# Six adaLN pieces of the second block: from TensorE chunks in the first half's up-projection to row products on GpSimd and ScalarE

## The chip, the cores and the metric

The kernel runs on one core of a Trainium2 chip. The metric is device time of one execution in microseconds (us), as the median of several runs. Besides, one execution was taken by the hardware profiler; all durations below come from it. Its engines are named PE (TensorE), PEld (PE's weight loads), DVE (VectorE), ACT (ScalarE), POOL (GpSimd) and SP (the sync engine, which here only issues DMAs). Each engine works through its own list of instructions in order.

## The reference, cut to what matters

Two layers on 256 context and 256 latent tokens of width 1024. Each layer computes six adaLN vectors per conditioning vector, and they scale and shift every norm and gate every residual:

```
mod_l = (silu(c) @ mod_w[layer] + mod_b[layer])       # 6 x 1024 values for the latent tokens
mod_c = (silu(c_ctx) @ mod_w[layer] + mod_b[layer])   # the same for the context tokens
sh1, sc1, g1, sh2, sc2, g2 = split(mod, 6)
h = rmsnorm(x, norm_mix_g) * (1 + sc1) + sh1 ;  x = x + g1 * mixer(h)
h = rmsnorm(x, norm_ffn_g) * (1 + sc2) + sh2 ;  x = x + g2 * conv_ffn(h)
```

The second layer is the last one, so from `g1` on it needs the latent vector alone. `conv_ffn` is an up-projection to 2 x 2816 channels, a depthwise convolution, SiLU gating and a down-projection.

## The kernel before, in words

Activations lie transposed: 128 channels on the partitions, 512 tokens along a row (`xT`, eight tiles). Every large product is made of three matmuls on split operands: a weight unit of eight 128x128 blocks is loaded by SP into `raw`, rounded by ACT into `wh` (L173), and the rest is formed into `wl` by DVE or POOL (L174). `Stream` does this one unit ahead; `wp` keeps four units. A unit of eight blocks serves 24 matmuls of 512 columns (L185 to L187).

A chunk (`mod_chunk(l, j)`) makes 512 columns of the adaLN product: two loads of 1 MB, eight matmuls with a 32-column operand (L244), a copy by ACT (L261), four transposes (L264), and two or three small DVE operations. Twelve chunks make a layer; chunks 4 and 5 of layer 1 are `g1`, 6 and 7 are `sh2`, 8 and 9 are `sc2`. In the kernel before, nine chunks of layer 1 are taken from the list `fill1` by the first feed-forward's up-projection, one for each 16 blocks from the third load on.

The first feed-forward has two halves. In each, eleven steps `project(jj)` make a gate tile and a value tile (two units of weights, 48 matmuls), `centre` copies each off the accumulators (ACT, L792), DVE adds the other taps (L798), ACT and POOL finish the gating (L816, L819, L822, L823); then comes that half's down-projection.

Ahead of it stands the first out-projection (`WO`, eight units): four row tiles together, then four one by one. After each, DVE adds the residual (L334), ACT squares it (L286) and DVE adds up the squares (L288); after the eighth square follow a column sum on PE, a chain of small DVE operations, the transposes of L140 and the copy of the result on ACT (`rstd`, L141). Only then can the norm (L315, L321, L323) feed the up-projection.

What order the instructions take on each engine is decided by a scheduler when the program is built: it goes by dependencies and by its own durations, not by the source's order alone. It is fixed in the built program.

Of the kernel before, what the change touches and what calls it, by code (L numbers as in the profile page):

```python
# [51 lines left out]
def block_kernel(ctx: ExitStack, tc: tile.TileContext, A: dict, out: bass.AP):  # L52
# [91 lines left out]
    class Stream:  # L144
        def __init__(self, src, nblocks, fill=None, every=1, skip=0, ahead=1, pool=rawp, eng=lambda u: v, parts=wp):


            self.src, self.n, self.ahead, self.parts = src, nblocks, ahead, parts
            self.fill, self.every, self.skip, self.pool, self.eng = fill, every, skip, pool, eng
            self.raw = self.rawi = None  # L150
            self.units = {}

        def load(self, d):
# [10 lines left out]
        def split(self, u):  # L164
            self.load(u // 2)
            if u == 1:
                nc.sync.dma_start(out=self.raw[:, 1024:], in_=self.src[0, :, 1024:])
            n = min(8, self.n - u * 8) * P
            o = (u % 2) * 1024
            hi = self.parts.tile([P, 1024], F32R, tag="wh", name=nm("wh"))  # L170
            lo = self.parts.tile([P, 1024], F32R, tag="wl", name=nm("wl"))
            rw = self.raw[:, o:o + n]
            s.activation(out=hi[:, :n], in_=rw, func=AF.Copy)  # L173
            self.eng(u).tensor_tensor(out=lo[:, :n], in0=rw, in1=hi[:, :n].bitcast(F32), op=ALU.subtract)  # L174
            self.units[u] = (hi, lo)

        def get(self, b):
            u = b // 8
# [79 lines left out]
    def mod_out(l, c, n, ps, psa):  # L258

        ev = t2((P, n * P))  # L260
        s.copy(out=ev, in_=ps)  # L261
        pt = psa()[:, :n * P].rearrange("p (a b) -> p a b", b=P)
        for a in range(n):
            te.transpose(pt[:, a, :], ev[:, a * P:(a + 1) * P], ident)  # L264
        col = lambda name, o: pc(name, o, n).unsqueeze(2).to_broadcast([P, n, 2])
        i, k = c // KD, c % KD
        dst = comps[l][i][:, k:k + n, :]
        v.tensor_reduce(out=dst, in_=pt.rearrange("p a (q c) -> p a c q", q=4)[:, :, 0:2, :], axis=AX.X, op=ALU.add)
        v.tensor_tensor(out=dst, in0=dst, in1=col("modb", l * 48 + c), op=ALU.add)
        if i in (1, 4):  # L270

            v.scalar_tensor_tensor(out=dst, in0=dst, scalar=1.0, in1=col("nmg" if i == 1 else "nfg", l * 8 + k), op0=ALU.add, op1=ALU.mult)

    accs = np_.tile([P, T], F32, tag="acc", name="acc", bufs=1)

# [100 lines left out]

        acts = norm_mod(0, 0, 1, SEGS, r, start)
    fill0 = [lambda j=j: mod_chunk(0, j) for j in (4, 5, 8, 9, 6, 7)]
    fill1 = [lambda j=j: mod_chunk(1, j) for j in (3, 0, 1, 4, 5, 8, 9, 6, 7, 11)]
    E.fill0, E.W0 = fill0, W0  # L380
    nrm = Norm(0, T)
    with ExitStack() as st:
        even_mixer(E, st, acts, pss0, nrm.add)
    for k in range(KD):
        dump(f"x1_{k}", xT[k])
    r = nrm.row()
    mod_chunk(1, 2, rawp, mps)
    acts = norm_mod(0, 3, 4, SEGS, r)
    with ExitStack() as st:
        hs, nrms = [], [Norm(a, b) for _, a, b in SEGS]  # L390

        def then(m, sgs):
            for sg in sgs:
                nrms[sg[0]].add(m)
                if m == KD - 1:
                    hs[:] = hs or [htiles(k) for k in range(KD)]
                    norm_mod(1, 0, 1, (sg,), nrms[sg[0]].row(), tiles=hs)

        conv_ffn(E, st, acts, fill1[:-1], then)
    for k in range(KD):  # L400
        dump(f"x2_{k}", xT[k])
    with ExitStack() as st:
# [8 lines left out]
        last_ffn(E, st, acts, fill1[-1:], out)  # L411


def even_mixer(E, st, acts, pss0, then):
    nc, tc, A = E.nc, E.tc, E.A
    v, s, g, te = E.v, E.s, E.g, E.te
    pc, nm, mps, dump, ident, ones = E.pc, E.nm, E.mps, E.dump, E.ident, E.ones
# [348 lines left out]
    finish(3)  # L766
    for k in range(8):
        dump(f"m{k}", hh[k].bitcast(F32))
    WO = E.Stream(A["wout0"], 64)
# [56 lines left out]
def conv_ffn(E, st, acts, fill, then):  # L826

    v, g = E.v, E.g
    cv = Conv(E, st, 0, T)
# [1 line left out]
    up = E.Stream(E.A["up0"], 44 * KD, fill, 1, 2, pool=ur, eng=lambda u: g)  # L831
    first = []
    per = FF // 2
    dn = E.Stream(E.A["dn0"], FF * KD, eng=lambda u: g if u * 8 % (per * KD) < per * 4 else v)

    def project(j):
        if j == 0:
# [10 lines left out]
    for hf in range(2):  # L848
# [6 lines left out]
        for jj in range(per):  # L855
            cg, ca = nxt
            if jj < per - 1:
                nxt = project(hf * per + jj + 1)

            if jj == per - 2:  # L860
                done = jj - 1
                pss = E.gemm_k(dn, b0, per, oa, [(0, T)] * 4, pss, range(done))
            h, part = cv.tile(cg, ca, g, part, jj)
            hm.append(h)
        part()
        last = hf == 1
# [4 lines left out]
        for m in range(4, KD - 2 if last else KD):  # L871
            E.residual(0, 5, m, E.gemm_f(dn, b0 + m * per, per, oa), SEGS)
            if last:
                then(m, SEGS)

    for sg in SEGS:
        for m in (KD - 2, KD - 1):
# [373 lines left out]
def layout(inp):  # L1251
# [2 lines left out]
    xx = np.concatenate([f["ctx"][0], f["x"][0]], 0)  # L1254
    A["x"] = xx.T.reshape(KD, P, T).transpose(1, 0, 2).reshape(P, KD * T)
    A["cv"] = np.stack([f["c_ctx"], f["c"][0]], -1).reshape(KD, P, 2).transpose(1, 0, 2).reshape(P, 16)
    A["mods"] = f["mod_w"][0][:, :2048].reshape(KD, P, 8, 256).transpose(2, 1, 0, 3).reshape(8, P, 2048)
    A["modw"] = f["mod_w"].reshape(2, KD, P, 12, 512).transpose(0, 3, 2, 1, 4).reshape(2, 12, P, 4096)
    prm = np.zeros((P, NPRM), np.float32)
# [106 lines left out]
```

## Time before, and its profile

| | us |
|---|---|
| median of three runs (1280.5 to 1283.16) | 1280.86 |
| the profiled execution | 1282.09 |
| its span, first to last instruction | 1280.3 |
| PE busy | 1227.8 (96%) |
| DVE, ACT, POOL busy | 926.0, 594.4, 428.8 |

The profiled execution is 1.23 us above the median; 1.8 us of it lie outside the span.

### The profile page before, as it was taken

How to read it: one execution, taken by the hardware profiler on the slowest of the kernel's cores; microseconds unless marked ns; L12 is line 12 of the kernel's file. 1: busy time of each engine (PE TensorE's matmuls, PEld its weight loads, DVE VectorE, ACT ScalarE, POOL GpSimd, SP SyncE). 2: the span in 40 equal slices, each digit the busy share in tenths (PEclk: the TensorE clock that was granted, in tenths of full speed). 3: DMA queues.
4: the chain of work that ended last, by engine and by line, in shares of the span. 5: the costliest groups of instructions: out<-in, count | busy, mean ns of one | idle time of the engine just before them, and what ended most of it. 6: DMA issues, size and time to landing. Idle time of an engine off the chain costs nothing.

```text
span 1280.3 us, 18746 instructions
## 1 busy us (share of the span) xinstructions
PE 1227.8 (96%) x7094; PEld 1003.9 (78%) x7094; DVE 926.0 (72%) x2061; ACT 594.4 (46%) x937; POOL 428.8 (33%) x249
## 2 busy tenths in 40 slices
PE   7989999999999999999999999999999998999995
PEld 5657787876867777888888897888888897899994
DVE  4483889487658776227785478888888956989995
ACT  4463345344344333223443346666666645555543
POOL 0100000000225565326666000032222224999974
PEclk8999999999999999999999999999999998999998
DMA  9557202334536564222211225453544376555521
GB/s 372 200 187 234 107 22 78 129 107 165 172 130 263 202 259 166 99 99 99 99 66 66 99 75 147 142 168 124 165 131 125 108 270 218 193 172 191 178 91 61
DMA packets 40106, 191.45 MB, mean 150 GB/s; under 512 B 4608, under 2 KB 10568, under 8 KB 21072
## 3 DMA queue, kind: packets, MB, share of 16 engines
q1 hardware_dynamic: 36512, 185.48, 41.6%
q10 hardware_dynamic: 3504, 4.77, 1.2%
q8 instruction: 56, 0.92, 0.3%
q14 instruction: 34, 0.28, 0.1%
HBM read 189.03 MB, written 1.20 MB: 149 GB/s over the span
## 4 chain that ended last, share of the span: by engine, by line
PE 75%; DVE 10%; issue 4%; DMA 4%; ACT 4%; POOL 2%; SPq 0%; DVEq 0%; ACTq 0%; POOLq 0%
PE gps L185 12%; PE gps L186 12%; PE gps L187 12%; PE mps L185 6%; PE mps L187 6%; PE mps L186 6%; PE vps L244 3%; PE gps L932 1%; PE vps L1174 1%; PE gps L933 1%; PE gps L931 1%; POOL wl L174 1%; PE gps L220 1%; PE gps L222 1%; PE gps L221 1%
## 5 line engine op out<-in xcount | busy, mean ns | idle before, releaser
L174 POOL TENSOR_TENSOR wl<-raw,wh 128x1024 fp32r<-128x1024 f32 x122 | 293.6, 2415 | 495.7 <-ACT wh L173 459.4
L173 ACT ACTIVATE wh<-raw 128x1024 fp32r<-128x1024 f32 x226 | 237.4, 1054 | 170.8 <-PE gps L187 99.6
L185 PE MATMUL gps<-hh,wh 128*128 128x512 f32 (+1 forms) x824 | 290.8, 354 | 6.7 <-ACT hh L321 4.9
L186 PE MATMUL gps<-hh,wl 128*128 128x512 f32 (+1 forms) x824 | 289.6, 352 | 1.1 <-DVE wl L174 1.1
L187 PE MATMUL gps<-hl,wh 128*128 128x512 f32 (+1 forms) x824 | 290.2, 353 | 0.0
L798 DVE SCALAR_TENSOR_TENSOR y<-mps,fcw,y 128x255 f32<-128x255 f32 (+3 forms) x592 | 247.5, 433 | 51.7 <-ACT y L792 37.5
L185 PEld LDWEIGHTS gps<-hh,wh 128*128 128x128 f32 x824 | 155.6, 189 | 41.7 <-issue 12.5
L174 DVE TENSOR_TENSOR wl<-raw,wh 128x1024 fp32r<-128x1024 f32 x104 | 127.6, 1234 | 79.6 <-ACT wh L173 79.4
L185 PE MATMUL mps<-hh,wh 128*128 128x256 f32 (+1 forms) x544 | 178.2, 328 | 0.0
L187 PE MATMUL mps<-hl,wh 128*128 128x256 f32 (+1 forms) x544 | 176.5, 325 | 1.6 <-DVE hl L323 1.6
L186 PE MATMUL mps<-hh,wl 128*128 128x256 f32 (+1 forms) x544 | 177.0, 325 | 0.0
L186 PEld LDWEIGHTS gps<-hh,wl 128*128 128x128 f32 x824 | 156.1, 189 | 23.2 <-issue 3.2
L187 PEld LDWEIGHTS gps<-hl,wh 128*128 128x128 f32 x824 | 156.0, 190 | 20.8 <-issue 1.7
L185 PEld LDWEIGHTS mps<-hh,wh 128*128 128x128 f32 x544 | 105.4, 194 | 16.9 <-issue 6.7
L187 PEld LDWEIGHTS mps<-hl,wh 128*128 128x128 f32 x544 | 105.2, 194 | 9.2 <-DVE hl L323 1.8
L186 PEld LDWEIGHTS mps<-hh,wl 128*128 128x128 f32 x544 | 105.6, 194 | 7.8
L798 DVE SCALAR_TENSOR_TENSOR y<-gps,fcw,y 128x189 f32<-128x189 f32 (+3 forms) x180 | 77.7, 438 | 22.0 <-ACT y L792 18.2
L792 ACT ACTIVATE y<-mps,fcw 128x256 f32<-128x256 f32 (+1 forms) x68 | 41.2, 637 | 91.5 <-PE mps L187 91.5
L185 PE MATMUL gps<-mh,wh 128*128 128x512 f32 (+1 forms) x198 | 73.5, 371 | 0.0
L187 PE MATMUL gps<-ml,wh 128*128 128x512 f32 (+1 forms) x198 | 73.4, 371 | 0.0
L186 PE MATMUL gps<-mh,wl 128*128 128x512 f32 (+1 forms) x198 | 73.4, 370 | 0.0
L334 DVE SCALAR_TENSOR_TENSOR x<-gps,mod,x 128x256 f32<-128x256 f32 x56 | 24.2, 478 | 42.0 <-PE gps L187 42.0
(292 smaller groups left out, 1894.0 us busy)
## 6 DMA issues: line engine op xcount, KB each, us to landing
raw<-in_up SPq DMA_DIRECT2D x42, 1024.0 KB, 4.9
rawm<-in_modw SPq DMA_DIRECT2D x36, 1024.0 KB, 6.6
raw<-in_win SPq DMA_DIRECT2D x32, 1024.0 KB, 5.4
raw<-in_dn SPq DMA_DIRECT2D x20, 1024.0 KB, 5.1
raw<-in_wout SPq DMA_DIRECT2D x10, 1024.0 KB, 5.6
rawm<-in_mods SPq DMA_DIRECT2D x8, 1024.0 KB, 14.5
R<-crd SPq DMA_DIRECT2D x32, 256.0 KB, 4.2
rawm<-in_modw SPq DMA_DIRECT2D x8, 512.0 KB, 5.0
```

What stands on the lines that cost most here:

```text
L173: s.activation(out=hi[:, :n], in_=rw, func=AF.Copy)
L174: self.eng(u).tensor_tensor(out=lo[:, :n], in0=rw, in1=hi[:, :n].bitcast(F32), op=ALU.subtract)
L185: te.matmul(out=ps, lhsT=lhi, rhs=rhi, start=first, stop=False)
L186: te.matmul(out=ps, lhsT=llo, rhs=rhi, start=False, stop=False)
L187: te.matmul(out=ps, lhsT=lhi, rhs=rlo, start=False, stop=last)
L220: te.matmul(out=ps, lhsT=ah[:, sl], rhs=hi[:, c:c + 512], start=k == 0, stop=False)
L221: te.matmul(out=ps, lhsT=ah[:, sl], rhs=lo[:, c:c + 512], start=False, stop=False)
L222: te.matmul(out=ps, lhsT=al[:, sl], rhs=hi[:, c:c + 512], start=False, stop=k == nk - 1)
L244: te.matmul(out=ps[32 * (k % 4):32 * (k % 4) + 32, :], lhsT=spad[:, k, :], rhs=raw[:, kk * 512:(kk + 1) * 512], start=k < 4, stop=k >= 4)
L334: v.scalar_tensor_tensor(out=xT[m][:, a:b], in0=ps[:, a - base:b - base], scalar=gt[:, m, ci:ci + 1], in1=xT[m][:, a:b], op0=ALU.mult, op1 ...
L792: self.E.s.activation(out=y, in_=ps, func=AF.Identity, scale=self.fcw[:, c + 4:c + 5], bias=self.fcw[:, c + 9:c + 10])
L798: self.E.v.scalar_tensor_tensor(out=o, in0=i, scalar=self.fcw[:, ti * 10 + wi:ti * 10 + wi + 1], in1=o, op0=ALU.mult, op1=ALU.add)
```

## The change

Chunks 4 to 9 of layer 1 leave `fill1`. In their place the class `Rows` makes these 3072 values for the latent vector in 24 pieces of 128: `start()` loads `c` to all partitions (`row`), forms silu(c) there with ACT and POOL, and each `step()` does three things for three pieces: ACT sums the products of one piece along its row (an activation copy with a summing output, L299), SP loads 512 KB of transposed weights for a new piece (`wt`, two buffers, L308), and POOL multiplies the loaded piece by `row` (L313). `start` and the steps hang on units of the first out-projection (6 steps), on units of both halves' down-projection and on odd steps of the second half's up-projection; what is left is made at the end. The out-projection moves out of the mixer's scope, so that the new pool takes over memory of the mixer. In each half two more units of the down-projection are split by DVE in place of POOL.

```diff
+            if self.aside:
+                self.aside(u)
...
+        def start(self):
+            pool = self.pool
+            self.row = pool.tile([P, D], F32, tag="row", name="row")
+            nc.sync.dma_start(out=self.row, in_=A["crow"].to_broadcast([P, D]))
+            th = pool.tile([P, D], F32, tag="wt", name=nm("wt"), bufs=2)
+            s.activation(out=th, in_=self.row, func=AF.Tanh, scale=0.5)
+            g.tensor_scalar(out=th, in0=th, scalar1=0.5, scalar2=0.5, op0=ALU.mult, op1=ALU.add)
+            g.tensor_tensor(out=self.row, in0=self.row, in1=th, op=ALU.mult)
...
+                s.activation(out=w, in_=w, func=AF.Copy, accum_out=dst[:, k, 1:2])
...
+                w = self.pool.tile([P, D], F32, tag="wt", name=nm("wt"), bufs=2)
+                nc.sync.dma_start(out=w, in_=A["modt"][self.c])
...
+                g.tensor_tensor(out=self.made[1], in0=self.made[1], in1=self.row, op=ALU.mult)
...
-    fill1 = [lambda j=j: mod_chunk(1, j) for j in (3, 0, 1, 4, 5, 8, 9, 6, 7, 11)]
+    fill1 = [lambda j=j: mod_chunk(1, j) for j in (3, 0, 1, 11)]
...
+    WO.aside = lambda u: rows.start() if u == 1 else rows.step() if u > 1 else None
...
-    dn = E.Stream(E.A["dn0"], FF * KD, eng=lambda u: g if u * 8 % (per * KD) < per * 4 else v)
+    dn = E.Stream(E.A["dn0"], FF * KD, eng=lambda u: g if u % per < 4 else v)
+    dn.aside = lambda u: rows.step() if u % per >= 4 else None
...
+            if jj % 2 and hf:
+                rows.step()
...
+    rows.finish()
```

ACT at the end of the out-projection, before: `wh` are rounded weight units of the up-projection (`raw_3152` its first load), `t<-x` the squares of residual tiles 4 to 7 (x_95 the last), then a chunk's copy and `rstd`.

```order
L286 ACTIVATE t_547_2906<-x_92 128x512
L173 ACTIVATE wh_3159<-raw_3152 128x1024
L286 ACTIVATE t_552_2942<-x_93 128x512
L173 ACTIVATE wh_3189<-raw_3187 128x1024
L286 ACTIVATE t_556_2976<-x_94 128x512
L173 ACTIVATE wh_3217<-raw_3187 128x1024
L286 ACTIVATE t_558_3006<-x_95 128x512
L261 COPY t_569_3055<-mps_3042 128x512
L141 COPY rstd_3022<-vps_3036 128x512
```

The same place now, from the square of tile 5; L299 sums a piece, and the squares' line is L332.

```order
L332 ACTIVATE t_558_2970<-x_93 128x512
L299 ACTIVATE wt_2941,mod_2_114<-wt_2941 128x1024
L299 ACTIVATE wt_2979,mod_2_114<-wt_2979 128x1024
L173 ACTIVATE wh_3219<-raw_3217 128x1024
L332 ACTIVATE t_563_3008<-x_94 128x512
L299 ACTIVATE wt_4293,mod_2_114<-wt_4293 128x1024
L173 ACTIVATE wh_3247<-raw_3217 128x1024
L299 ACTIVATE wt_4378,mod_2_114<-wt_4378 128x1024
L332 ACTIVATE t_565_3038<-x_95 128x512
L263 COPY t_576_3085<-mps_3072 128x512
L299 ACTIVATE wt_4412,mod_3_115<-wt_4412 128x1024
L141 COPY rstd_3052<-vps_3066 128x512
```

Eight sums stand ahead of the last square and a ninth ahead of `rstd`; `wt_4293`, `wt_4378` and `wt_4412` hang on the first half's down-projection in the source.

POOL from its first work of this stretch, before: the rests of the up-projection's first units.

```order
L174 TENSOR_TENSOR wl_3155<-raw_3152,wh_3154 128x1024
L174 TENSOR_TENSOR wl_3160<-raw_3152,wh_3159 128x1024
L174 TENSOR_TENSOR wl_3190<-raw_3187,wh_3189 128x1024
L174 TENSOR_TENSOR wl_3218<-raw_3187,wh_3217 128x1024
L174 TENSOR_TENSOR wl_3271<-raw_3245,wh_3270 128x1024
```

POOL at the same place now: the row of silu(c) (L290, L291), then products of pieces (L313) between those rests.

```order
L290 TENSOR_SCALAR wt_2752<-wt_2752 128x1024
L291 TENSOR_TENSOR row<-row,wt_2752 128x1024
L313 TENSOR_TENSOR wt_2786<-wt_2786,row 128x1024
L313 TENSOR_TENSOR wt_2816<-wt_2816,row 128x1024
L174 TENSOR_TENSOR wl_3185<-raw_3182,wh_3184 128x1024
L313 TENSOR_TENSOR wt_2850<-wt_2850,row 128x1024
L313 TENSOR_TENSOR wt_2901<-wt_2901,row 128x1024
L174 TENSOR_TENSOR wl_3190<-raw_3182,wh_3189 128x1024
L313 TENSOR_TENSOR wt_2941<-wt_2941,row 128x1024
L313 TENSOR_TENSOR wt_2979<-wt_2979,row 128x1024
L174 TENSOR_TENSOR wl_3220<-raw_3217,wh_3219 128x1024
L313 TENSOR_TENSOR wt_4293<-wt_4293,row 128x1024
```

Two products stand before each rest of a unit; further down the list the 24th and last product stands ahead of the rest of the up-projection's sixteenth unit, in the first half.

ACT between the norm and the first `centre` copies of the up-projection, before: two roundings, a chunk's copy, then the copies.

```order
L173 ACTIVATE wh_3332<-raw_3245 128x1024
L173 ACTIVATE wh_3385<-raw_3361 128x1024
L261 COPY t_614_3260<-vps_3247 128x512
L792 ACTIVATE y_3298<-gps_3148,fcw_3143 128x512
L792 ACTIVATE y_3300<-mps_3149,fcw_3143 128x512
```

The same place now, where the copies' line is L847 and the chunk's copy L263.

```order
L299 ACTIVATE wt_4454,mod_3_115<-wt_4454 128x1024
L173 ACTIVATE wh_3362<-raw_3275 128x1024
L299 ACTIVATE wt_4491,mod_3_115<-wt_4491 128x1024
L299 ACTIVATE wt_4523,mod_3_115<-wt_4523 128x1024
L173 ACTIVATE wh_3415<-raw_3391 128x1024
L263 COPY t_621_3290<-vps_3277 128x512
L847 ACTIVATE y_3328<-gps_3178,fcw_3173 128x512
L299 ACTIVATE wt_4560,mod_3_115<-wt_4560 128x1024
L847 ACTIVATE y_3330<-mps_3179,fcw_3173 128x512
```

Three sums now stand ahead of the chunk's copy, and a fourth between the first two `centre` copies.

## Rows read from the trace of the kernel before

**Rows 1.** The page: the span, busy time of each engine.

```profile
span 1280.3 us, 18746 instructions
PE 1227.8 (96%) x7094; PEld 1003.9 (78%) x7094; DVE 926.0 (72%) x2061; ACT 594.4 (46%) x937; POOL 428.8 (33%) x249
```

**Rows 2.** Windows: start:end, length, busy of PE, PEld, DVE, ACT, POOL; clock, DMA.

```profile
440.00:460.00 20.00, 20.00 (x99) 15.15 (x98) 12.80 (x31) 7.25 (x10) 9.79 (x5) 1.00 0.52 203
...
540.00:560.00 20.00, 20.00 (x87) 16.10 (x86) 5.37 (x8) 4.25 (x4) 1.39 (x1) 1.00 0.31 105
...
600.00:620.00 20.00, 20.00 (x90) 16.53 (x89) 15.58 (x37) 8.99 (x12) 12.99 (x9) 1.00 0.30 105
```

**Rows 3.** Timeline, ACT: start, duration; `centre` copies in the first and second half.

```profile
455.61 0.78 ACT L792 ACTIVATE y<-mps,fcw 128x512 f32<-128x512 f32 x1 [1.02 <-PE mps L187]
...
469.07 0.78 ACT L792 ACTIVATE y<-mps,fcw 128x512 f32<-128x512 f32 x1 [1.02 <-PE mps L187]
...
590.49 0.78 ACT L792 ACTIVATE y<-mps,fcw 128x512 f32<-128x512 f32 x1 [3.19 <-PE mps L187]
...
601.37 0.78 ACT L792 ACTIVATE y<-mps,fcw 128x512 f32<-128x512 f32 x1 [3.19 <-PE mps L187]
```

**Rows 4.** Timeline, PE: a chunk inside the up-projection.

```profile
447.48 1.92 PE L244 MATMUL vps<-rawm,spad 128*32 128x512 f32 x16
449.33 0.50 PE L185 MATMUL mps<-hh,wh 128*128 128x512 f32 x1
```

**Rows 5.** Timeline, SP: the up-projection's first load.

```profile
320.51 0.33 SPq L159 DMA_DIRECT2D raw<-in_up  x1
```

**Rows 6.** DMA issues: KB each, median us from issue to landing.

```profile
raw<-in_win SPq DMA_DIRECT2D x6, 512.0 KB, 3.5
...
raw<-in_wout SPq DMA_DIRECT2D x4, 512.0 KB, 4.4
...
raw<-in_dn SPq DMA_DIRECT2D x4, 512.0 KB, 5.8
```

**Rows 7.** Lines by form, POOL and ACT: count, busy, mean ns, idle before.

```profile
L174 POOL TENSOR_TENSOR wl<-raw,wh 128x1024 fp32r<-128x1024 f32 x122 | 293.6, 2415 | 495.7 <-ACT wh L173 459.4 <-DVE acc L288 33.1 <-issue 2.1
L823 POOL TENSOR_TENSOR ml<-y,mh 128x512 fp32r<-128x512 f32 x22 | 28.6, 1301 | 2.2 <-ACT mh L822 2.2
...
L1163 POOL TENSOR_TENSOR CE<-CE 128x256 f32<-128x256 f32 x16 | 24.1, 1508 | 63.2 <-DVE CE L1162 63.2
L823 POOL TENSOR_TENSOR ml<-y,mh 128x256 fp32r<-128x256 f32 x22 | 16.3, 741 | 7.6 <-ACT mh L822 7.6
...
L1038 POOL TENSOR_SCALAR cl<-cl 128x256 f32<-128x256 f32 x4 | 3.5, 880 | 111.2 <-DVE cum L1063 82.1 <-PE mps L1032 29.1
```

**Rows 8.** Timeline, ACT: from the out-projection's last squares to the first chunk's copy.

```profile
337.04 1.06 ACT L173 ACTIVATE wh<-raw 128x1024 fp32r<-128x1024 f32 x1 [3.02 <-PE gps L187]
...
353.37 1.06 ACT L173 ACTIVATE wh<-raw 128x1024 fp32r<-128x1024 f32 x1 [3.87 <-PE gps L187]
354.34 0.61 ACT L286 ACTIVATE t<-x 128x512 f32<-128x512 f32 x1
...
359.85 0.59 ACT L141 COPY rstd<-vps 128x512 f32<-128x512 f32 x1 [1.07 <-PE vps L140]
...
376.02 0.51 ACT L321 ACTIVATE hh<-t,mod 128x256 fp32r<-128x256 f32 x1 [0.28 <-DVE t L315]
...
382.15 0.59 ACT L261 COPY t<-vps 128x512 f32<-128x512 f32 x1 [0.83 <-PE vps L244]
```

**Rows 9.** Timelines, DVE and POOL: an addition of squares without and beside POOL's work.

```profile
335.09 0.69 DVE L288 TENSOR_TENSOR acc<-acc,t 128x512 f32<-128x512 f32 x1
...
338.65 2.54 DVE L288 TENSOR_TENSOR acc<-acc,t 128x512 f32<-128x512 f32 x1 [0.79 <-ACT t L286]
...
338.24 2.40 POOL L174 TENSOR_TENSOR wl<-raw,wh 128x1024 fp32r<-128x1024 f32 x1 [286.77 <-ACT wh L173]
```

**Rows 10.** Timeline, PE: the first chunk's transposes in the up-projection.

```profile
383.01 0.60 PE L264 MATMUL vps<-c,t 128*128 128x128 f32 x4
```

More of the change, by code (lines that the diff above doesn't have):

```diff
@@ L149, in __init__ @@
             self.fill, self.every, self.skip, self.pool, self.eng = fill, every, skip, pool, eng
-            self.raw = self.rawi = None
+            self.raw = self.rawi = self.aside = None
             self.units = {}
@@ L272, in mod_out, with __init__, step, finish @@
             v.scalar_tensor_tensor(out=dst, in0=dst, scalar=1.0, in1=col("nmg" if i == 1 else "nfg", l * 8 + k), op0=ALU.add, op1=ALU.mult)
+    class Rows:
+        N = 3 * KD
+        def __init__(self, pool):
+            self.pool, self.c, self.loaded, self.made = pool, 0, None, None
+        def start(self):
[6 more added lines that the diff above has]
+            g.tensor_tensor(out=self.row, in0=self.row, in1=th, op=ALU.mult)
+        def step(self):
+            if self.made is not None:
+                c, w = self.made
+                i, k = 2 + c // KD, c % KD
+                dst = comps[1][i]
+                s.activation(out=w, in_=w, func=AF.Copy, accum_out=dst[:, k, 1:2])
+                if k == KD - 1:
+                    d = dst[:, :, 1]
+                    v.tensor_tensor(out=d, in0=d, in1=pc("modb", 48 + 8 * i, 8), op=ALU.add)
+                    if i == 4:
+                        v.scalar_tensor_tensor(out=d, in0=d, scalar=1.0, in1=pc("nfg", 8, 8), op0=ALU.add, op1=ALU.mult)
+            new = None
+            if self.c < self.N:
+                w = self.pool.tile([P, D], F32, tag="wt", name=nm("wt"), bufs=2)
+                nc.sync.dma_start(out=w, in_=A["modt"][self.c])
+                new = (self.c, w)
+                self.c += 1
+            self.made = self.loaded
+            if self.made is not None:
+                g.tensor_tensor(out=self.made[1], in0=self.made[1], in1=self.row, op=ALU.mult)
+            self.loaded = new
+        def finish(self):
+            while self.loaded or self.made:
+                self.step()
     accs = np_.tile([P, T], F32, tag="acc", name="acc", bufs=1)
@@ L382, in block_kernel @@
     with ExitStack() as st:
-        even_mixer(E, st, acts, pss0, nrm.add)
+        hh, hl = even_mixer(E, st, acts, pss0)
+    mst = ExitStack()
+    rows = Rows(mst.enter_context(tc.tile_pool(name="mw", bufs=1)))
+    even_out(E, hh, hl, nrm.add, rows)
     for k in range(KD):
@@ L388, in block_kernel @@
     acts = norm_mod(0, 3, 4, SEGS, r)
-    with ExitStack() as st:
+    with mst, ExitStack() as st:
         hs, nrms = [], [Norm(a, b) for _, a, b in SEGS]
@@ L397, in then @@
                     norm_mod(1, 0, 1, (sg,), nrms[sg[0]].row(), tiles=hs)
-        conv_ffn(E, st, acts, fill1[:-1], then)
+        conv_ffn(E, st, acts, fill1[:-1], then, rows)
     for k in range(KD):
@@ L411, in block_kernel, with even_mixer @@
         last_ffn(E, st, acts, fill1[-1:], out)
-def even_mixer(E, st, acts, pss0, then):
+def even_mixer(E, st, acts, pss0):
     nc, tc, A = E.nc, E.tc, E.A
@@ L768, in even_mixer, with even_out @@
         dump(f"m{k}", hh[k].bitcast(F32))
-    WO = E.Stream(A["wout0"], 64)
+    return hh, hl
+def even_out(E, hh, hl, then, rows):
+    WO = E.Stream(E.A["wout0"], 64)
+    WO.aside = lambda u: rows.start() if u == 1 else rows.step() if u > 1 else None
     oa = lambda k: (hh[k], hl[k])
@@ L823, in tile, with conv_ffn @@
         return (h_, l_), lambda: self.E.g.tensor_tensor(out=l_, in0=ya, in1=h_.bitcast(F32), op=ALU.subtract)
-def conv_ffn(E, st, acts, fill, then):
+def conv_ffn(E, st, acts, fill, then, rows):
     v, g = E.v, E.g
@@ L1256, in layout @@
     A["cv"] = np.stack([f["c_ctx"], f["c"][0]], -1).reshape(KD, P, 2).transpose(1, 0, 2).reshape(P, 16)
+    A["crow"] = f["c"].reshape(1, D)
+    A["modt"] = f["mod_w"][1][:, 2048:2048 + 3 * D].T.reshape(3 * KD, P, D)
     A["mods"] = f["mod_w"][0][:, :2048].reshape(KD, P, 8, 256).transpose(2, 1, 0, 3).reshape(8, P, 2048)
```

## The prediction

> **What bounds the kernel now.** I read the page first: PE is busy 1227.8 of 1280.3 us [rows 1], so time comes off only where PE has less to do, and goes on wherever PE is made to wait. Then windows inside the stretches that the change touches: PE is busy 20.00 of 20 us in the first half's up-projection (440 to 460), in the first down-projection (540 to 560) and in the second up-projection (600 to 620) [rows 2]. The other engines have room there, POOL 9.79, 1.39 and 12.99 of 20, ACT 7.25, 4.25 and 8.99. Between the out-projection and the up-projection it is the other way round: the chain square, sum of squares, `rstd`, norm runs on ACT, DVE and POOL, and PE has nothing to multiply until it ends. The timeline of ACT gives its marks: last square at 354.34, `rstd` at 359.85, the last `hh` at 376.02, the first chunk's copy at 382.15 [rows 8]. Whatever delays one of these marks delays the end.
>
> **What is gained.** Six chunks leave PE. In the first half, where each step holds a chunk, two `centre` copies of the value tile stand 469.07 - 455.61 = 13.46 us apart; in the second half, without chunks, 601.37 - 590.49 = 10.88 [rows 3]. The difference is 2.58 us, and it is plausible: 1.85 of it lie between the start of a chunk's matmuls and the next matmul of the projection [rows 4], the rest is its transposes. 6 x 2.58 = 15.5 us gained. The second number also gives PE's need for one unit of weights: 10.88 / 2 = 5.44.
>
> **What is added, and where it stands.** 24 products of 128x1024 on POOL, 24 sums on ACT. For a product the nearest row is POOL's `wl`, two operands of the same shape, 2.415 us [rows 7]; for a sum ACT's rounding of the same shape, 1.06 with start-up [rows 8]. That is 58 us of POOL and 25 of ACT, which the whole feed-forward could hide. But the built order does not spread them over it: eight sums stand ahead of the last square, a ninth ahead of `rstd`, and all 24 products ahead of the rest of the sixteenth unit of the first half's up-projection. Engines work in order, so each piece standing ahead of a mark has to be loaded, multiplied and summed before it.
>
> *First term, the last square.* I follow the chain. The row's load can start when the memory of the mixer is read out; the up-projection's first load, which stood there before, was issued at 320.51 [rows 5]. A load of 512 KB lands after 3.5 to 5.8 us, middle 4.4 [rows 6]: 324.9 (the row is a load to all partitions and so of this size). Tanh on ACT 1.05 and a handover between engines of about 0.1 (a rounding that starts at 337.04 and lasts 1.06 is followed by its `wl` at 338.24 [rows 8, 9]): 326.1. The operation with two constants on 1024 columns is not in the trace; bounds are 2.41, the two-operand form of the same size, and 3.5, four times the 0.88 of the same kind on 256 columns [rows 7]; I take 3.0, between them: 329.2. The product of the row 2.41: 331.6. Piece 0, loaded meanwhile: product to 334.0, sum to 335.2. The second buffer was the tanh's, and is free for piece 1 only at 331.6: load to 336.1, product 338.6, sum 339.7. From there the two buffers make a ring. ACT does a rounding, POOL its `wl` and then two products, ACT two sums; the next rounding stands behind those sums, and the next `wl` waits for it. First round: two roundings 2.1, `wl` 2.4, two products 4.8, a sum 1.05, handovers: pieces 2 and 3 are done at 350.9. Each later round is 1.05 + 2.41 + 2 x 2.41 + 1.05 + four handovers 0.4 = 9.7: pieces 4 and 5 at 360.6, 6 and 7 at 370.3. Loads of 4.4 fit in the round, since a buffer is free when its sum ends. Then the square, 0.61, ends at 371.0 against 354.95 before: **+16.0** (12 with short loads, the low bound of the constant operation and some overlap of the rounds; 19 with the upper bounds). What decides it is that a round takes 9.7 and a unit of PE 5.44.
>
> There is a rule that speaks against the 3.0: the Trainium skill, "GPSIMD Engine Reference", section "4.1 Engine selection", calls operations with one input roughly line-rate on GpSimd; with the 128 values per cycle of its section 3 that is an estimate of some 0.9 us for 1024 columns, and the first term would be 2 us less. The row of 0.88 for 256 columns [rows 7] does not look like that, and the sum goes by the row.
>
> *Second term, `rstd`.* Piece 8's product and sum stand between the last square and `rstd`. The sum waits for the product, which starts as the ring lets it, about when the square does. The rest of the chain on DVE can be held by POOL: an addition of squares takes 0.69 alone, and 2.54 when it starts beside a `wl` of 2.40 [rows 9]. Together **+1.5** (0 to 2.5).
>
> *Third term, from `rstd` to PE.* Before, the last `hh` ended 376.02 + 0.51 - 359.85 = 16.7 after `rstd` started [rows 8]. Pieces 9 and 10 are multiplied within this stretch and hold DVE for up to 2 x 2.41: 21.5. Three sums stand ahead of the first chunk's copy on ACT, and the last of them, of piece 11, needs the buffer of piece 9: its sum after the norm 1.05, load 4.4, product 2.41, sum 1.05, then a rounding 1.05 and the copy 0.6, so the copy ends some 32.3 after `rstd`, before 382.15 + 0.59 - 359.85 = 22.9. PE's transposes of this chunk stand right behind the copy (383.01) [rows 10], and PE works in order, so all matmuls behind them wait too: 9.4, and 4.6 if the norm stays as fast as it was and piece 9 is summed earlier. I take **+7.5** (4 to 9).
>
> *Fourth term, POOL in the up-projection.* From the fourteenth piece to the last, POOL's list holds 11 products, 8 `wl`, and 10 of the 512-column subtractions and products of the gating, 1.30 each [rows 7]: 26.6 + 19.3 + 13.0 = 58.9 us busy. PE's need for the same eight units, with two chunks left, is 8 x 5.44 + 2 x 2.58 = 48.7. So at least +10. It is more when POOL waits for ACT: at each of eight places a `wl` stands behind products whose sums stand ahead of its rounding, a sum, a rounding and three handovers, 2.4 each, 19 if none of it is covered. Between 10 and 29, nearer to the first, as some sums fall beside POOL's gating: **+15**.
>
> *At nothing:* four more units of the down-projection on DVE, 5.37 of 20 us busy there [rows 2]; a unit's rest would have to be later than the 5.44 us that its predecessor gives. The sums' small additions on DVE, 8 columns wide, lie in the same cover. The 24 loads are 12 MB in place of the chunks' 12 MB; DMA is half used [rows 2]. In the second half nothing is left to do.
>
> **The sum.** 16.0 + 1.5 + 7.5 + 15 - 15.5 = +24.5. The profiled execution took 1282.09, so 1306.6 for one like it; it stands 1.2 above the median of the runs, so I predict 1305. All low ends: 12 + 0 + 4 + 10 - 15.5 = +10.5, 1291; all high ends, with 25 for the last term: 19 + 2.5 + 9 + 25 - 15.5 = +40, 1321, which I hold unlikely since waits overlap (a late norm gives POOL time to get ahead).
>
> **The rivals.** *The pieces are hidden (other side, faster).* If a round of two pieces took no longer than a unit of PE, 5.44, ACT would never be late with a square, and the gain alone would show: 1280.9 - 15.5 = 1265. For it: ACT and POOL have the time in sum. Against: the round holds three POOL operations of 2.41, 7.2 without any wait; products would have to take less than (5.44 - 2.41 - 2.5) / 2 = 0.3 us, or run ahead of the square's round, which the order and two buffers don't allow. It would also need up-projection work of POOL below 48.7 instead of 58.9. Chance 0.07.
>
> *The norm is not late, but the up-projection is POOL-bound.* If the row is ready much sooner than I work out (its load not waiting for the mixer) and the eight pieces fit in the out-projection, the first two terms fall away: 7.5 + 15 - 15.5 = +7, 1288. Against it is that out-projection units are only 5.44 apart and the ring 9.7. Chance 0.15, with the cases between.
>
> *POOL's operations get longer beside DVE.* A 256-column POOL operation takes 1.508 in one place and 0.741 in another [rows 7], so a busy neighbour can double it. If ten of the products beside the norm and the gating take 0.8 more, +8: 1313. The products would have to meet DVE's two-operand work each time. Chance 0.10. Beside this: the Trainium skill, "SBUF — State Buffer", section "Who interferes with whom", says that a DVE operation with two SBUF inputs and a GpSimd operation that reads share one port pair, and that whoever starts first holds it for its whole instruction; the addition of 2.54 [rows 9] agrees, and by that rule DVE would delay POOL as much as POOL delays DVE.
>
> **How the numbers follow.** The forecast, all four terms at about their size, has 0.68. The range of 1287 to 1317 takes in the second and third rival and the low ends, and leaves out the first rival and the highest ends. A measurement of this kernel can tell about 0.2%, 2.6 us, from no change. Slower: 0.68 + 0.10 + most of the second rival, 0.85. Faster: the first rival and a little for low ends together with a larger gain, 0.10. Same: the rest, 0.05.
>
> **What would show it.** First term: the last square at about 371 in place of 354.3, with L299 and the `wl` of POOL alternating before it, and the `wt` loads waiting for sums. Third: the first `centre` copy some 24 us later than before, and PE idle at the chunk's transposes. Fourth: idle time of PE on `wl` of POOL in the first half's up-projection, and the last L313 well inside that half. Gain: steps without a chunk 10.88 apart once POOL has finished. I am wrong if the square of tile 7 stays near 355, or if products take well under 2.4; and wrong in size if the loads land faster than 3.5 or the row is loaded before 320.

## The result, and the profile after

The changed kernel takes 1303.66 us (median of four runs, 1303.51 to 1309.29) against 1280.88 before: a ratio of 1.0159, with a 95% interval of 1.0127 to 1.0191. By the medians it is slower by 22.8 us, and by the interval of the ratio by 16 to 24 us; 1305 was predicted. The profiled execution took 1303.61, with a span of 1301.7, 21.4 more than in [rows 1].

The page, span and busy time of each engine after the change (as [rows 1]):

```profile
span 1301.7 us, 18617 instructions
PE 1224.2 (94%) x6974; PEld 1004.7 (77%) x6974; DVE 940.8 (72%) x2055; ACT 616.7 (47%) x980; POOL 481.3 (37%) x271
```

PE has 120 instructions less, six chunks of 16 matmuls and 4 transposes (the eight matmuls of a chunk in the source stand as 16 in the trace), but its busy time fell by 3.6 us only, and its idle time rose from 52.5 to 77.5.

ACT's timeline after the change, with the marks of [rows 8] (the squares' line is now L332, a sum is L299, the norm's `hh` L367, the chunk's copy L263, `centre` L847):

```profile
321.64 0.69 ACT L787 ACTIVATE hh<-mps,c 128x512 fp32r<-128x512 f32 x1 [4.27 <-PE mps L786]
...
351.27 1.04 ACT L173 ACTIVATE wh<-raw 128x1024 fp32r<-128x1024 f32 x1
352.22 0.62 ACT L332 ACTIVATE t<-x 128x512 f32<-128x512 f32 x1
357.57 1.06 ACT L299 ACTIVATE wt<-wt 128x1024 f32<-128x1024 f32 x1 [4.74 <-POOL wt L313]
...
359.88 1.06 ACT L299 ACTIVATE wt<-wt 128x1024 f32<-128x1024 f32 x1 [1.16 <-POOL wt L313]
...
360.94 1.04 ACT L173 ACTIVATE wh<-raw 128x1024 fp32r<-128x1024 f32 x1
...
370.57 0.61 ACT L332 ACTIVATE t<-x 128x512 f32<-128x512 f32 x1
...
376.88 0.58 ACT L141 COPY rstd<-vps 128x512 f32<-128x512 f32 x1 [1.44 <-PE vps L140]
...
396.85 0.51 ACT L367 ACTIVATE hh<-t,mod 128x256 fp32r<-128x256 f32 x1 [0.28 <-DVE t L361]
...
406.38 0.56 ACT L263 COPY t<-vps 128x512 f32<-128x512 f32 x1
411.14 0.78 ACT L847 ACTIVATE y<-gps,fcw 128x512 f32<-128x512 f32 x1 [4.20 <-PE gps L189]
...
596.78 0.78 ACT L847 ACTIVATE y<-gps,fcw 128x512 f32<-128x512 f32 x1 [4.40 <-PE gps L189]
```

The reader sees the ring: a rounding at 351.27 and a square, then ACT idle for 4.74 until the first product, a sum, idle for 1.16, a sum, and the next rounding at 360.94, 9.67 later. The second sum of the next pair ends 9.63 after that of this pair, though there the rounding stands between the two sums. The last square ends at 371.18, 16.2 later than before, of which 1.2 lie ahead of the mixer's end. The last row is the first `centre` copy of the second half, 22.61 later than before.

The same three marks in the trace of before, which [rows 8] don't have: the mixer's last `hh`, and the first `centre` copy of each half.

```profile
320.41 0.69 ACT L738 ACTIVATE hh<-mps,c 128x512 fp32r<-128x512 f32 x1 [4.27 <-PE mps L737]
...
386.18 0.78 ACT L792 ACTIVATE y<-gps,fcw 128x512 f32<-128x512 f32 x1 [3.44 <-PE gps L187]
...
574.17 0.78 ACT L792 ACTIVATE y<-gps,fcw 128x512 f32<-128x512 f32 x1 [4.40 <-PE gps L187]
```

POOL's timeline after the change, the row (L290, L291) and one round of the ring:

```profile
328.44 1.05 POOL L290 TENSOR_SCALAR wt<-wt 128x1024 f32<-128x1024 f32 x1 [278.66 <-ACT wt L289]
329.58 3.26 POOL L291 TENSOR_TENSOR row<-row,wt 128x1024 f32<-128x1024 f32 x1
...
352.39 2.40 POOL L174 TENSOR_TENSOR wl<-raw,wh 128x1024 fp32r<-128x1024 f32 x1 [2.21 <-ACT wh L173]
354.75 5.09 POOL L313 TENSOR_TENSOR wt<-wt,row 128x1024 f32<-128x1024 f32 x2
```

POOL waits for the rounding, ACT for the products, and neither works ahead of the other. Over the whole kernel ACT stood for a product 17 times, 51.7 us in all.

DVE's timeline in the norm: the first operation behind the sum of squares, and the lower halves of the norm tiles (L369), one alone and three in one row:

```profile
372.62 1.67 DVE L112 TENSOR_SCALAR rm<-most 128x4 f32<-128x4 f32 x1
...
384.63 0.48 DVE L369 SCALAR_TENSOR_TENSOR hl<-t,mod,hh 128x256 fp32r<-128x256 f32 x1
...
387.36 7.47 DVE L369 SCALAR_TENSOR_TENSOR hl<-t,mod,hh 128x256 fp32r<-128x256 f32 x3 [1.05 <-ACT hh L367]
```

POOL works without a gap from 387.06 to 394.56, on a rest and two products: three operations of DVE that take 0.48 alone take 7.47 there. The operation on 4 columns, 1.67 here, took 0.43 before.

The longest of what PE waited for between 345 and 540 (engine, line, total us, times, longest); in the trace of before there are two waits, of 2.0 and 0.8 us:

```profile
PE vps L266 <- ACT t L263: 11.2, 3, 6.4
PE vps L132 <- DVE acc L334: 10.5, 1, 10.5
PE mps L188 <- POOL wl L174: 1.9, 1, 1.9
```

The 10.5 are the late squares as PE meets them: its last matmul of the out-projection starts at 354.12, as early as before from the mixer's end, and then it stands until 365.00 for the sum of squares.

Windows of 10 us at the end of the out-projection (columns as in [rows 2]):

```profile
350.00:360.00 10.00, 4.51 (x20) 3.38 (x19) 3.26 (x3) 3.89 (x7) 7.64 (x4) 0.87 0.67 216
360.00:370.00 10.00, 5.00 (x20) 2.35 (x20) 3.36 (x4) 5.08 (x8) 7.95 (x4) 0.50 0.40 110
```

PE is idle about half of the time, and its granted clock, 0.87 in the first window, is 0.50 in the second, the lower of its two levels. The matmuls that follow take longer too: of the first ones of the up-projection three, from 379.6 to 380.5, take 0.63 us each, those from 381.6 on 0.40.

### The profile page after: what moved, and what is told of

It is laid out like the page before. It is cut to its first block, busy times and chain, and to the rows that moved or that the text cites. A ratio compares the mean times of both kernels' runs of the same rounds, so it can differ in the third digit from the quotient of the medians.

```text
span 1301.7 us, 18617 instructions
## 1 busy us (share of the span) xinstructions
PE 1224.2 (94%) x6974; PEld 1004.7 (77%) x6974; DVE 940.8 (72%) x2055; ACT 616.7 (47%) x980; POOL 481.3 (37%) x271
## 3 DMA queue, kind: packets, MB, share of 16 engines
q10 hardware_dynamic: 3504, 4.77, 1.2%
## 4 chain that ended last, share of the span: by engine, by line
PE 50%; POOL 5%; DVE 4%; issue 4%; ACT 4%; DMA 1%; DVEq 0%; SPq 0%; POOLq 0%; ACTq 0%
PE gps L187 8%; PE gps L188 8%; PE gps L189 8%; PE mps L189 5%; PE mps L188 5%; PE mps L187 5%; POOL wl L174 3%; ACT wh L173 1%; PE gps L991 1%; POOL wt L313 1%; PE vps L1233 1%; PE gps L992 1%; PE gps L990 1%; PE vps L1220 1%; PE mps L1186 1%
## 5 line engine op out<-in xcount | busy, mean ns | idle before, releaser
L174 POOL TENSOR_TENSOR wl<-raw,wh 128x1024 fp32r<-128x1024 f32 x118 | 284.1, 2418 | 183.6 <-ACT wh L173 131.9
L174 DVE TENSOR_TENSOR wl<-raw,wh 128x1024 fp32r<-128x1024 f32 x108 | 132.9, 1237 | 75.3 <-ACT wh L173 75.2
L290 POOL TENSOR_SCALAR wt<-wt 128x1024 f32<-128x1024 f32 x1 | 1.1, 1052 | 278.7 <-ACT wt L289 278.7
L847 ACT ACTIVATE y<-mps,fcw 128x256 f32<-128x256 f32 (+1 forms) x68 | 41.0, 634 | 78.1 <-PE mps L189 78.1
```

The lines of the kernel that those rows point to most:

```text
L847: self.E.s.activation(out=y, in_=ps, func=AF.Identity, scale=self.fcw[:, c + 4:c + 5], bias=self.fcw[:, c + 9:c + 10])
```

## The experiments

Theory: the pieces cost where they stand ahead of work that PE waits for, in the four places of the prediction, and six chunks less give 15.5. Rivals: the pieces cost wherever they stand (their loads, POOL beside DVE, the pool over the mixer's memory), or PE loses only at the chunk's transposes, or two buffers are too few. When the mixer ends, ahead of all that was edited, the profiled executions stand between 319.95 and 324.64, so stages are compared by their lengths. These are differences of times in ACT's timeline: M is the start of the mixer's last `hh` copy, S the end of the last square, R, C and D the starts of `rstd`, of the first `centre` copy of the first half and of that of the second half. Each line is one profiled execution.

| | M to S | S to R | R to C | C to D | D to end |
|---|---|---|---|---|---|
| before | 34.54 | 4.90 | 26.33 | 187.99 | 706.1 |
| changed | 49.54 | 5.70 | 34.26 | 185.64 | 704.9 |
| no pieces | 34.53 | 4.91 | 26.34 | 172.52 | 704.7 |
| no sums | 34.71 | 6.63 | 37.61 | 180.79 | 708.9 |
| after the norm | 34.54 | 4.90 | 34.36 | 198.92 | 707.1 |
| chunks late | 48.85 | 6.06 | 35.17 | 179.72 | 712.0 |
| held late | 34.53 | 4.91 | 24.72 | 171.17 | 705.5 |
| held at the source's places | 36.86 | 8.00 | 26.31 | 172.27 | 704.6 |
| no products | 36.76 | 4.55 | 26.29 | 173.13 | 704.4 |
| three buffers | 51.11 | 8.12 | 36.79 | 184.81 | 707.8 |

Four of them ran beside a kernel before of 1283.17 us (median), the other four beside one of 1284.68; the ratios are to these.

**No pieces.** The 24 pieces are left out and their values set to a constant; all else is as changed, the units of the down-projection that DVE took over too.

```diff
+    for i in (2, 3, 4):
+        v.memset(comps[1][i][:, :, 1], 0.5)
...
-    WO.aside = lambda u: rows.start() if u == 1 else rows.step() if u > 1 else None
...
-    dn.aside = lambda u: rows.step() if u % per >= 4 else None
...
-            if jj % 2 and hf:
-                rows.step()
...
-    rows.finish()
```

Expected: 

> The six chunks are gone and the 24 pieces are not computed at all (the three vectors are set to a constant), all else as changed. Theory of the order (the whole loss comes from the pieces, the whole gain from six chunks of 2.58 us): 1280.9 - 15.5 = 1265.4, within 2; the last square ends near 355 as before, and 22.6 us between this run and the changed kernel at the end of the first half become some 38. Rival (the chunks were cover for other waits, so that the gain was smaller, and the losses too): above 1270.

Measured: 1265.63 us, ratio 0.9859 (0.9834 to 0.9885). ACT's timeline, first `centre` copy of each half:

```profile
385.73 0.78 ACT L848 ACTIVATE y<-gps,fcw 128x512 f32<-128x512 f32 x1 [3.45 <-PE gps L189]
...
558.25 0.78 ACT L848 ACTIVATE y<-gps,fcw 128x512 f32<-128x512 f32 x1 [4.39 <-PE gps L189]
```

C to D is 172.52, 15.47 less than before: the gain is what six chunks were taken to be worth. The stages from M to C are as they were, to 0.01 us; D to end is 1.4 shorter, which is within what that stage differs by from kernel to kernel. PE has as many instructions as in the changed kernel (6974) and is busy 1210.3 us of a span of 1262.9. Of the 38.8 us by which the changed kernel's span is longer, 13.9 are therefore the same number of PE instructions taking longer, and 24.9 are idle time. Of the 13.9, 2.1 lie ahead of M, 3.3 between M and R, 2.4 between R and C, 6.4 between C and D. The last is seen in the windows from C to D, of the changed kernel and then of this one (columns as in [rows 2]):

```profile
411.14:596.78 185.64, 178.89 (x770) 142.14 (x770) 110.42 (x251) 73.48 (x102) 108.87 (x57) 0.97 0.39 136
385.73:558.25 172.52, 172.52 (x770) 138.38 (x769) 107.90 (x247) 60.96 (x77) 83.40 (x45) 1.00 0.35 124
```

The same 770 instructions of PE take 6.37 us more, and PE is idle for 6.75 where it was never idle without the pieces.

**No sums.** Besides the sums, the small additions on DVE behind them are left out; the values are a constant.

```diff
             if self.made is not None:
...
-                s.activation(out=w, in_=w, func=AF.Copy, accum_out=dst[:, k, 1:2])
...
+                pass
```

Expected: 

> Loads and products stay, the 24 sums on ScalarE are left out (the three vectors are set to a constant). Theory of the order as predicted: what holds the last square is a rounding that stands behind sums that wait for products; without sums ScalarE waits for nothing there, and the square ends between 355 and 362. GpSimd's list keeps some two products ahead of each rest of a unit, so the up-projection still loses at least 10 to GpSimd: 1265.4 + 10 to 18, so 1275 to 1283. Rival 1 (the products alone, or their loads, hold the out-projection): near 1300. Rival 2 (all of the fourth term is the chunk's copy behind sums, none of it GpSimd's list): 1266 to 1269.

Measured: 1288.72 us, ratio 1.0040 (1.0015 to 1.0065); the runs scatter from 1279.79 to 1295.11 and the profiled one is the slowest, so the lengths of the stages are what counts. ACT's and then DVE's timeline:

```profile
358.74 0.61 ACT L329 ACTIVATE t<-x 128x512 f32<-128x512 f32 x1
365.98 0.59 ACT L141 COPY rstd<-vps 128x512 f32<-128x512 f32 x1 [2.79 <-PE vps L140]
...
396.98 0.51 ACT L364 ACTIVATE hh<-t,mod 128x256 fp32r<-128x256 f32 x1 [0.28 <-DVE t L358]
```

```profile
369.89 7.61 DVE L358 SCALAR_TENSOR_TENSOR t<-x,mod,rstd 128x256 f32<-128x256 f32 x3
...
378.22 0.47 DVE L358 SCALAR_TENSOR_TENSOR t<-x,mod,rstd 128x256 f32<-128x256 f32 x1
```

The square is not late at all (M to S 34.71), which bears the theory out for the first term. The expected time was missed for another reason: with ACT out of the way, POOL runs a rest and products straight through the norm and holds DVE twice (three operations in 7.61 us, and three more in 7.41 at 387.55), so that the last `hh` ends 31.5 after `rstd` in place of 16.7. C to D is 8.3 longer than without pieces. What PE waited for there:

```profile
PE vps L268 <- ACT t L265: 4.0, 1, 4.0
PE vps L248 <- DMA rawm<-in_modw: 1.4, 1, 1.4
```

The 4.0 go back to POOL's list: the chunk's copy on ACT, at 432.58, stands behind a gating operation that waited 6.59 us for POOL, and POOL, with products ahead of its gating, was busy for 10.00 and 9.86 of the 10 us before and behind 430. The 1.4 are a wait for a chunk's weights, and the remaining 2.9 are PE's instructions taking longer (175.44 us for the same 770). So of the 8.3 POOL's list alone accounts for 4.0 of waiting; how the 2.9 divide between the two waits is not shown.

**After the norm.** The row waits for the last norm tile, and the out-projection's six steps stand behind the first projection of the first half.

```diff
+            v.tensor_scalar(out=half, in0=after, scalar1=0.0, scalar2=0.5, op0=ALU.mult, op1=ALU.add)
...
-            s.activation(out=th, in_=self.row, func=AF.Tanh, scale=0.5)
+            s.activation(out=th, in_=self.row, func=AF.Tanh, scale=half[:, 0:1])
...
+    rows.start(acts(7)[0][:, 511:512].bitcast(F32))
...
-    WO.aside = lambda u: rows.start() if u == 1 else rows.step() if u > 1 else None
...
+        if not hf:
+            for _ in range(6):
+                rows.step()
```

Expected: 

> The row of silu(c) is held back by one small operation that reads the last norm tile, so that no product and no sum can start before the norm is done; nothing else changes in what is computed. Theory of the order: the last square and rstd are as before (355 and 360), 17.0 us come back, but all 24 products now stand in the first half's up-projection: GpSimd has 24 x 2.41 + 22 x 2.41 + 22 x 1.30 = 139.5 us there where TensorE needs 11 x 10.88 + 2 x 2.58 = 124.8, so another 5 to 15 are lost there: 1292 to 1302. Rival 1 (only the place at the out-projection costs; the up-projection hides the rest): 1287 or less. Rival 2 (the new memory pool or the loads cost, not the order): the square stays late.

Measured: 1303.32 us, ratio 1.0141 (1.0115 to 1.0167), not clear of the changed kernel (1.0127 to 1.0191) and just above what was expected. What PE waited for from 345 to 540:

```profile
PE mps L187 <- DVE y L855: 9.0, 2, 4.7
PE vps L266 <- ACT t L263: 8.5, 3, 5.3
PE gps L188 <- POOL wl L174: 4.4, 3, 1.9
PE mps L188 <- POOL wl L174: 2.5, 1, 2.5
```

The out-projection and `rstd` are as before, to 0.01 us, so what was lost there came from the pieces' place. The up-projection gives it all back: C to D is 26.4 longer than without pieces (19.2 of it PE idle), and C comes 8.0 late on the copy that stands behind sums. So the out-projection is not the only dear place: all 24 products crowd into the first half, from 386.5 to 526.9, ahead of work that PE waits for.

**Chunks late.**

```diff
-    fill1 = [lambda j=j: mod_chunk(1, j) for j in (3, 0, 1, 11)]
+    fill1 = [lambda j=j: mod_chunk(1, j) for j in (3,)] + [lambda: None] * 10 + [lambda j=j: mod_chunk(1, j) for j in (0, 1, 11)]
```

Expected: 

> Chunks 0 and 1 leave the first half's up-projection for the second half's; the pieces stay as changed. Theory of the fourth term as predicted (GpSimd's list is the bound of that stretch): the first half ends no earlier, and the second half gets 2 x 2.58 longer: 1303.7 to 1309. Rival (TensorE loses there at the chunks' transposes, which stand behind a copy that stands behind sums, 4.8 us of idle time in the changed kernel's trace, and at the low clock after each such stop): some 5 to 10 come back, 1294 to 1299.

Measured: 1304.13 us, ratio 1.0156 (1.0134 to 1.0179), as the changed kernel. PE's waits from 345 to 540:

```profile
PE vps L266 <- ACT t L263: 6.7, 1, 6.7
PE mps L188 <- POOL wl L174: 3.6, 2, 2.6
PE gps L188 <- POOL wl L174: 1.9, 1, 1.9
```

Two of the three stops at transposes are gone, and more stops on POOL's `wl` (5.5 us in place of 1.9) stand there instead. C to D fell by 5.9, of which 5.2 are the two chunks themselves, and D to end rose by 7.1. The rival falls, since the time did not come back: the transposes are only where PE notices that ACT and POOL are late.

**Held late.** Each sum reads, as its scale, a column that DVE makes from a tile of the place that the step hangs on (0 times the tile, plus 1), so that it can't be pulled ahead of that place. The row is held in the same way, and the places are new: none at the out-projection, the first in the first half's up-projection.

```diff
+                    v.tensor_scalar(out=one, in0=after, scalar1=0.0, scalar2=1.0, op0=ALU.mult, op1=ALU.add)
+                    s.activation(out=w, in_=w, func=AF.Identity, scale=one[:, 0:1], accum_out=dst[:, k, 1:2])
...
-    WO.aside = lambda u: rows.start() if u == 1 else rows.step() if u > 1 else None
...
+    dn.aside = lambda u, after: rows.step(after) if u in (2, 3, 4, 5, 6, 7, 8, 9, 10) or u - per in (2, 4, 6, 8) else None
...
+            if jj == 2 and not hf:
+                rows.start(h[0][:, 0:1].bitcast(F32))
+            elif jj % 2 and (hf or jj > 2):
+                rows.step(h[0][:, 0:1].bitcast(F32))
```

Expected: 

> All 24 pieces are computed, but each sum is held back by a tiny VectorE operation that reads a tile of the place it hangs on, so that the order can't pull it ahead; the first begins after the third gate tile of the first half, then one on every other step of both halves and on units of both down-projections, none at the out-projection or the norm. Theory of the order (the pieces cost only where they stand ahead of work that TensorE waits for): nearly the time without pieces, 1265.4 and up to 4 for a few waits, so 1265 to 1270. Rival (the pieces cost by what they do, their loads, GpSimd's work beside VectorE, wherever they stand): 1275 or more.

Measured: 1267.63 us, ratio 0.9876 (0.9842 to 0.9910): faster than both kernels, with all 24 pieces made. PE's waits from 345 to 540, and POOL's timeline around one piece in the second half:

```profile
PE gps L187 <- ACT hh L374: 2.0, 1, 2.0
PE mps L266 <- ACT t L263: 0.8, 1, 0.8
```

```profile
609.68 2.42 POOL L174 TENSOR_TENSOR wl<-raw,wh 128x1024 fp32r<-128x1024 f32 x1 [1.76 <-ACT wh L173]
612.77 2.40 POOL L320 TENSOR_TENSOR wt<-wt,row 128x1024 f32<-128x1024 f32 x1 [0.67 <-DMA wt<-in_modt]
...
616.37 2.44 POOL L174 TENSOR_TENSOR wl<-raw,wh 128x1024 fp32r<-128x1024 f32 x1
```

In this stretch PE waits as in the kernel before and nowhere else; behind it, up to 760, there is one wait of 1.4 us for a sum of squares that neither the kernel before nor the one without pieces has. R to C is even 1.6 shorter than before: PE's 109 instructions there take 22.70 us, at a granted clock of 1.00, where they took 24.30 at 0.94, and why the clock stayed up here is open. The piece fills POOL's idle time, and the rest behind it is still in time. The products now spread from 425.1 to 722.9. From M to the end this kernel takes 940.8 us, without pieces 943.0, so the same loads, products and sums cost nothing to speak of here, and the rival that they cost by what they are falls.

**Held at the source's places.** The same hold on the later sums, but the first six steps stay at the out-projection.

```diff
-    dn.aside = lambda u: rows.step() if u % per >= 4 else None
+    dn.aside = lambda u, after: rows.step(after) if u % per >= 4 else None
...
-                rows.step()
+                rows.step(h[0][:, 0:1].bitcast(F32))
```

Expected: 

> The places are those of the changed kernel's source, the out-projection's too, but each later sum is held at its place in the same way, so that only six pieces start at the out-projection. Theory of the order: four sums stand ahead of the last square in place of eight; these four were done at 352 in the changed kernel, one unit behind, and the two products after them may meet the norm: the square ends 3 to 6 late, the norm 0 to 5 longer, and the up-projection loses nothing: 1265.4 + 4 to 11, so 1269 to 1277. Rival (the start at the out-projection costs its 16 for the row, the pool over the mixer's memory or the loads alone): 1282 or more.

Measured: 1275.39 us, ratio 0.9939 (0.9917 to 0.9962), faster than before. ACT's timeline, last square and `rstd`:

```profile
358.58 0.63 ACT L337 ACTIVATE t<-x 128x512 f32<-128x512 f32 x1 [1.19 <-DVE x L385]
367.21 0.59 ACT L141 COPY rstd<-vps 128x512 f32<-128x512 f32 x1 [2.11 <-PE vps L140]
```

The square is 2.3 late and `rstd` another 3.1; nothing is lost behind it. The row, its load and the pool over the mixer's memory are all here, so they are not what cost 15. The rest of the loss came from later steps that the order had moved forward from where the source had hung them: four sums stand ahead of the last square here, eight in the changed kernel.

**No products.**

```diff
-                g.tensor_tensor(out=self.made[1], in0=self.made[1], in1=self.row, op=ALU.mult)
+                pass
```

Expected: 

> The 24 products on GpSimd are left out, the loads and the sums (of the raw weights) stay. Theory of the order: the sums are then late only by their loads, and GpSimd's list is that of the kernel without pieces. A round of two sums takes two loads that overlap, 4.4 + 2 x 1.25, about the 5.44 of a unit and a little more, so the square ends up to 5 late; no operation of VectorE in the norm is held; the up-projection loses 0 to 3: 1265.4 + 2 to 8, so 1267 to 1274. Rival (sums ahead of roundings are what costs, whatever makes them wait): 1285 or more.

Measured: 1271.10 us, ratio 0.9906 (0.9873 to 0.9940). The values are sums of the raw weights. ACT's timeline:

```profile
359.38 0.61 ACT L332 ACTIVATE t<-x 128x512 f32<-128x512 f32 x1
364.54 0.58 ACT L141 COPY rstd<-vps 128x512 f32<-128x512 f32 x1 [0.74 <-PE vps L140]
...
390.83 0.76 ACT L847 ACTIVATE y<-gps,fcw 128x512 f32<-128x512 f32 x1
```

Eight sums stand ahead of the last square again, but the square is only 2.2 late, the norm is as long as before, and C to D 0.6 longer than without pieces. Products alone make the square late by 0.2, sums alone by 2.2, and both by 15.0: at the square the price is in ACT and POOL waiting for each other in turn, not in either's work.

**Three buffers.**

```diff
-                w = self.pool.tile([P, D], F32, tag="wt", name=nm("wt"), bufs=2)
+                w = self.pool.tile([P, D], F32, tag="wt", name=nm("wt"), bufs=3)
```

Expected: 

> As changed, with three buffers for the pieces in place of two. Theory of the order: a round at the out-projection is a rounding, a rest, two products and a sum, 9.7 us of work that waits for itself and not for a load, and GpSimd's list is as long as before; a third buffer lets still more products stand ahead of the norm: no gain, 1300 to 1310. Rival (the two buffers and the loads behind sums make the rounds long): the square ends near 360 and the time is 1290 or less.

Measured: 1310.81 us, ratio 1.0211 (1.0172 to 1.0249). There is no gain; whether it is slower than the changed kernel (1.0127 to 1.0191) is not clear by the ratios, though the three stages from M to C are 1.6, 2.4 and 2.5 longer. POOL's timeline:

```profile
354.11 2.34 POOL L174 TENSOR_TENSOR wl<-raw,wh 128x1024 fp32r<-128x1024 f32 x1 [2.21 <-ACT wh L173]
356.41 5.10 POOL L313 TENSOR_TENSOR wt<-wt,row 128x1024 f32<-128x1024 f32 x2
363.71 2.34 POOL L174 TENSOR_TENSOR wl<-raw,wh 128x1024 fp32r<-128x1024 f32 x1 [2.20 <-ACT wh L173]
```

The round is 9.60 long with a third buffer, 9.67 with two, so the loads and the second buffer did not set it.

## Why the prediction was right

Measured by the table, the changed kernel's 21.4 us of span are: M to S +15.0, S to R +0.8, R to C +7.9, C to D -2.35, which is +13.1 of loss and -15.5 of gain, and +1.2 ahead of M and -1.2 behind D, where no piece stands in the built order. The total is right, and so in the main is the mechanism up to the first `centre` copy. The fourth term came out near its size in part by luck: nearly half of it is a cost that the prediction does not name.

- *Gain*, 15.5: 15.47 in the kernel without pieces.
- *First term*, 16.0: 15.0 from the mixer's end. The round was worked out at 9.7 and is 9.67 and 9.63. In what leads up to it three sizes were off and nearly cancelled, which is luck: the operation with two constants took 1.05, not 3.0, the product of the row 3.26, not 2.41, and the row's load, issued at 321.75, let ACT start only at 327.23, where 324.9 was put for its landing. The Trainium skill, "GPSIMD Engine Reference", section "4.1 Engine selection", was nearer on the first of these: its line rate for one input gave an estimate of 0.9, and the row of 0.88 for 256 columns, by which the sum went, was a bad neighbour.
- *Second term*, 1.5: 0.8. The operation of 1.67 at 372.62 lies beside the product of piece 8.
- *Third term*, 7.5: 7.2 to the end of the chunk's copy (30.06 after `rstd`, before 22.89), 7.9 to C. As predicted, products held DVE in the norm, the last `hh` ended 20.5 after `rstd` (21.5 predicted), and PE stopped at the chunk's transposes, for up to 6.4. The Trainium skill, "SBUF — State Buffer", section "Who interferes with whom", has whoever starts first hold the shared ports for its whole instruction; the three operations in 7.47 us, beside three of POOL in 7.5, agree. The third rival, in which POOL pays for this, hardly came: two products take 5.13 at the norm and 4.77 later in the up-projection, 0.2 more for each, and only the product of the row, 3.26, took clearly longer than its 2.38 to 2.41 in four other kernels. PE's instructions between R and C took 2.4 more than without pieces, so about 5.5 of the 7.9 are waiting.
- *Fourth term*, 15: 13.1, of which 6.75 are PE idle and 6.37 the same instructions taking longer. The prediction took all of it as PE waiting: at least 10 for POOL's list, and some 5 more where POOL waits for ACT. That list is as it was worked out: from the fourteenth product to the last POOL is busy 57.75 us, where 58.9 was said. But these take 74.1 us, in which ACT stands 27.3 us for products and POOL mostly for roundings, so it is not the list alone that bounds the stretch. Alone, without sums, it gave 4.0 us of waiting where "at least 10" was said; sums alone made C to D 0.6 longer. That the rest of the waiting comes from the two engines waiting for each other, as at the squares, is likely by this trace, but no run took it apart. PE showed it at transposes more than at `wl`, which the wording of what would show the step had not foreseen; the experiment with late chunks says that the place of the stop changes nothing.
- *Not in the prediction:* PE's clock, which it puts at nothing without a word. Against the kernel without pieces 13.9 us of the loss are PE instructions that took longer, 11.8 of them behind M; granted clocks of 0.50 and 0.87 in the windows where PE waits, and of 0.97 against 1.00 from C to D, fit that, though no run held the clock by itself. The 3.3 us ahead of `rstd` lie beside a wait that was there anyway. The 2.4 and 6.4 behind it add to the time. In the third and fourth terms together PE waited 12.3 in place of the 22.5 predicted, and 8.8 of the difference came back as slower instructions; that these nearly cancel is luck.

What stays open: each term was tested by leaving work out or moving it, and every such edit made a new order on all engines, so the share of single waits in the fourth term was not separated further. Nor was it tested how much of the loss would be left at an even clock.

## What to carry to other kernels

Where a scheduler places filler work, its place in the source says little: look at what stands ahead of each late mark in the built order, and price the loop of engines that wait for each other there, not their busy shares. Filler that crosses two engines (product on one, sum on the other) next to a stage that crosses the same two becomes a ring, here 9.7 us per round beside a need of 5.44. A data dependency that ties each piece to its place turned a loss of 1.6% into a gain of 0.6% with the source's places, and into a gain of 1.2%, at no cost that shows, with places behind the norm. And where PE waited, its instructions also took longer, here by 11.8 us behind the mixer's end: a sum of waits alone leaves that out.

## What the runs showed of the hardware

A POOL operation of two operands held DVE's operations one for one: three of 0.48 us took 7.47 beside 7.5 us of POOL, and one on 4 columns took 1.67, against 0.43 before. POOL itself lost 0.2 us for each product there (two in 5.13, later two in 4.77). POOL's operation with two constants on 1024 columns took 1.05 us, less than half of a product of the same size. At the end of the out-projection PE did nothing from 354.5 to 365.0; its granted clock was 0.50, the lower level, from 360 to 370, and the 6974 instructions of the changed kernel took 13.9 us more busy time than the same number without the pieces, 11.8 of it behind the mixer's end.
